# More buffers for key outputs and bias rows, the first gate loaded ahead of the last attention output, and the last merge parts moved forward on POOL

## The chip, the cores and the metric

The kernel runs on one core of a Trainium2 chip. The metric is the time of one launch on the device in microseconds (us). A core has five instruction queues that matter here: TensorE (PE, matmuls into PSUM banks), VectorE (DVE), ScalarE (ACT), GpSimd (POOL) and SyncE (SP, which here only issues transfers). Each runs its own list of instructions in order; semaphores tie them together. A tile with `bufs=n` has n buffers in turn, and whoever fills one again waits until the earlier use of that buffer is over, its transfer to memory included.

## The reference

One layer of a streaming encoder, for a new stream of 1024 frames and 64 more frames of a running one (1088 rows in all), in float32:

```
h = rms_norm(x, norm_w) @ w_in                    # 1024 -> 6144 columns
sb_q, sb_k, sb_v, sb_z, cb_q, cb_k, cb_v, cb_z, g_sb, g_cb = split(h)
o_sb = stick_breaking(sb_q, sb_k, sb_v)           # first branch, 8 heads x 64
o_cb = band_attention(cb_q, cb_k, cb_v, rel_bias) # second branch, 8 heads x 64
b_sb = (o_sb * silu(sb_z)) @ w_proj_sb
b_cb = (o_cb * silu(cb_z)) @ w_proj_cb
h = sigmoid(g_sb) * b_sb + sigmoid(g_cb) * b_cb   # the merge
y = x + h @ w_out
```

The new keys and values of both branches are outputs too.

## The kernel before, in words

Most float32 operands are split into two parts, a high part made by a copy on ACT to a shorter format (`whi`, `hl[:, 0]`, `og` with index 0) and a low part, the difference, made on DVE or POOL (`wlo`, `hl[:, 1]`, `og` with index 1). A product is then three matmuls: high by high, high by low, low by high. So each weight block goes through ACT and through DVE or POOL before PE can use it.

The work runs in five stages.

1. *First projection* (from L450), with frames on the partitions, for values and for the normalized queries and keys of the second branch. `make_rb` (L240) builds, in its eight calls, the bias rows of the eight heads: DVE writes a tile `rx` of 128 x 768 (L243, L244), and SP sends it to `d_rb` (L245). Between such calls DVE makes the low parts of the transposed queries and keys (L354), whose PSUM bank `pk` PE needs again (L349).
2. *Second projection* (L606 to L657), columns on the partitions, in pairs of weight blocks. Each pair takes seven products (s = 0 to 6) instead of eight, with sums of blocks (`s1`, `u2`, `u3`) added on DVE. `emit` (L565) splits a finished piece into `hl` and sends it to memory. For keys it also plans an `out` (L590): PE transposes the piece into a bank `acc` (L595, L597), ACT copies it into `ko` (L601) and, for the second column piece, into `kos` (L599), and SP sends both to the outputs. There are two `acc` banks, three `ko` and one `kos`. `soon(n, f)` puts f in a list, and `step` (L553), called once ahead of each product's matmuls, counts down and runs what has come due; with n = 1 that is the second `step` from there. The matmuls of a product are issued after `step`.
3. *Attention* of both branches, with the gate columns' projections put in as filling between steps (`fill`).
4. *Merge*. `proj_sb` (L855) multiplies the first branch's projection with its gate, and `proj_cb` (L894) does the same for the second branch in 12 jobs j: i, ci = divmod(j, 3), where i is the pair of weight blocks and ci one of three pieces of the frames (384, 384 and 320 columns). Before these jobs `load_og` (L822) fetches piece ci of the attention output (`ot`), and `make_og` (L842) splits it, four high parts on ACT (L834) and four low ones, alternately on POOL and DVE (L839). `load_gcb(j)` (L882) fetches gate j as two transfers of SP (L853), and `sig(j)` (L888) puts the sigmoid on ACT (L892, the first one loads the function table). Job j starts with `sig(j + 1)`, so that on ACT gate 1 stands ahead of the weights that are split after job 0 (L115 on ACT, L122 on DVE), which job 3 needs. After each job `keep_hi` (L931, on ACT, L937) and `keep_lo` (L939, on POOL, L945) split its result for the output projection. `sums_h` (L947) adds and splits pieces of the result (`tk`, L955 on ACT, L959 on DVE), for sums that the output projection multiplies.
5. *Output projection* (L1380 to L1463), again seven products in the order 0, 3, 2, 1, 4, "b", 5, 6. `prep_o` (L1243) splits its weights, on ACT (L1271) and POOL (L1272). `last_sums` (L1331), called while the first product runs, issues what is left of the merge: the remaining `sums_h`, the weights of the fourth product, and the parts of job 11. After them DVE adds results (L1432) and the rows of the running stream (L1449).

Of the kernel before, what the change touches and what calls it, by code (L numbers as in the profile page):

```python
# [32 lines left out]
def hybrid_step_kernel(ctx: ExitStack, tc: tile.TileContext, x_prompt, x_sample, c_sbk, c_sbv, c_cbk, c_cbv,  # L33
# [164 lines left out]
    with ExitStack() as ph:  # L198
# [40 lines left out]

        def make_rb(h):  # L240
            rb = rbs[0]
            rx = p1.tile([128, 768], F32, name="rx", bufs=2)
            V.tensor_scalar(rx[:, 0:512], rb[:, h, 256:257].to_broadcast([128, 512]), -1.0, None, op0=OP.mult)  # L243
            V.tensor_scalar(rx[:, 512:768], rb[:, h, 255::-1], -1.0, None, op0=OP.mult)  # L244
            SP.dma_start(d_rb[h], rx)  # L245
# [298 lines left out]
    with ExitStack() as ph:  # L544
# [5 lines left out]
        def soon(n, f):  # L550
            later.append([n, f])
# [13 lines left out]
        def emit(i, w, half, c, src, ps):  # L565

            kind, _, arg = pairs[i]
            n = XC[c][1] - XC[c][0]
            plain = lambda d, s: SP.dma_start(d, s)
            if kind in ("sig", "silu"):  # L570
                sg = up.tile([128, 2, 288], F32R, name="hl", bufs=HB)[:, 0].bitcast(F32)
                A.activation(sg[:, :n], src[:, :n], AF.Sigmoid)
                if kind == "silu":
                    V.tensor_tensor(out=sg[:, :n], in0=sg[:, :n], in1=src[:, :n], op=OP.mult)
                soon(0, lambda: stores(plain, half, c, sg[:, :n], arg[w][:]))
                return
            h = up.tile([128, 2, 288], F32R, name="hl", bufs=HB)
            A.activation(h[:, 0, :n], src[:, :n], AF.Copy)
            V.tensor_tensor(out=h[:, 1, :n], in0=src[:, :n], in1=h[:, 0, :n].bitcast(F32), op=OP.subtract)
            p = arg + w  # L580
            dst = (d_kT if kind == "k" else d_qT)["sb"][p]
            soon(0, lambda: stores(rdma, half, c, h[:, :, :n], dst[:]))
            if kind == "q":
                return
            kf = src
            if ps:
                kf = up.tile([128, 288], F32, name="kf", bufs=2)
                V.tensor_copy(kf[:, :n], src[:, :n])

            def out():  # L590
                pt = psF.tile([128, 512], F32, name="acc")
                ko = up.tile([128, 2, 128], F32, name="ko", bufs=3)
                cols = slice(p * 128, (p + 1) * 128)
                for t in range(2):
                    TE.transpose(pt[:, t * 128:(t + 1) * 128], kf[:, t * 128:(t + 1) * 128], ident)  # L595
                if c == 1:
                    TE.transpose(pt[:32, 256:384], kf[:, 256:288], ident)  # L597
                    kos = up.tile([32, 128], F32, name="kos", bufs=1)
                    A.activation(kos, pt[:32, 256:384], AF.Copy)  # L599
                    SP.dma_start(o_sbk_s[32 * half:32 * half + 32, cols], kos)  # L600
                A.activation(ko[:, :2], pt[:, :256].rearrange("p (t c) -> p t c", c=128), AF.Copy)  # L601
                a = half * 512 + c * 256
                SP.dma_start(o_sbk_p[a:a + 256, cols].rearrange("(t q) c -> q t c", q=128), ko[:, :2])
            soon(1, out)

        load_raw(2)  # L606
        for n in range(2, LEAD):
# [214 lines left out]
    def load_og(b, ci, stage, ps=range(NPAIR)):  # L822
        a, e = CH[ci]
        for p in ps:
            if b == "sb":
                ots[ci, p] = stage.tile([128, 384], F32, name="ot", bufs=4)
            elif p % 2 == 0:
                t = stage.tile([128, 2, 384], F32, name="ot", bufs=2)
                ots[ci, p], ots[ci, p + 1] = t[:, 0], t[:, 1]
            SP.dma_start(ots[ci, p][:, :e - a], d_o[b][p][:, a:e])  # L830
# [11 lines left out]
    def make_og(b, ci):  # L842
        for p in range(NPAIR):
            og_hi(b, ci, p)
            og_lo(b, ci, p)
# [36 lines left out]
    def load_gcb(j):  # L882
        if j < 12:
            i, ci = divmod(j, 3)
            load_gate(*((late["tbp"], "gt") if j % 4 < 2 else (late["y"], "ot")), ("cb", j),
                      (d_g["cb"][i], d_g["cb"][i + 4]), ci)

    def sig(j):  # L888
        if j < 12:
            a, e = CH[j % 3]  # L890
            t = gts["cb", j][:, :, :e - a]
            A.activation(t, t, AF.Sigmoid)  # L892
# [38 lines left out]
    def keep_hi(j):  # L931
        i, ci = divmod(j, 3)
        a, e = CH[ci]
        for u, z in ((i, 512), (i + 4, NP)):
            if a < min(e, z):
                hh, _, f = kept(u, a, min(e, z))
                A.activation(hh, f, AF.Copy)  # L937

    def keep_lo(j):  # L939
        i, ci = divmod(j, 3)  # L940
        a, e = CH[ci]
        for u, z in ((i, 512), (i + 4, NP)):
            if a < min(e, z):
                hh, hl, f = kept(u, a, min(e, z))
                G.tensor_tensor(out=hl, in0=f, in1=hh.bitcast(F32), op=OP.subtract)  # L945

    def sums_h(k):  # L947

        f, tk = late["tbt"], late["tk"][k]
        x = lambda h, c: f[:, k + 4 * h, 512 * c:512 * c + 512]  # L950
        d = [psF.tile([128, 512], F32, name="acc")[:] for _ in range(2)]

        def high(n):
            for j in range(2):
                A.activation(tk[:, 0, n + j], d[j], AF.Copy)  # L955

        def low(n):
            for j in range(2):
                V.tensor_tensor(out=tk[:, 1, n + j], in0=d[j], in1=tk[:, 0, n + j].bitcast(F32), op=OP.subtract)  # L959

        for j in range(2):
            V.tensor_tensor(out=d[j], in0=x(j, 1), in1=x(0, j), op=OP.subtract)
        high(0)
        yield
        low(0)
        V.tensor_tensor(out=d[1], in0=x(1, 1), in1=d[0], op=OP.subtract)
        V.tensor_tensor(out=d[0], in0=x(1, 0), in1=d[1], op=OP.subtract)
        yield
        high(2)
        yield  # L970
        low(2)
# [302 lines left out]

    late["o"] = prep_o
    for ci in range(3):
        load_og("cb", ci, late["y"])
        fill((46, 24, 100000)[ci])
        if ci == 2:
            for j in range(2):  # L1280
                load_gcb(j)
            late["h"][1] = [xpool.tile([128, 4, T], F32R, name=f"x{s}") for s in "ab"]
        make_og("cb", ci)
    sig(0)
    for j, q in enumerate(((0, 1), (1, 1), (0, 0))):
        SP.dma_start(wsum[j], w_quarter(0, *q))
    for j in range(2, 4):
# [43 lines left out]
    def last_sums():  # L1331
        for _ in tjobs:
            pass
        t3 = sums_h(3)
        for _ in range(3):
            next(t3)
        prep_o(3)
        keep_hi(11)
        keep_lo(11)
        for _ in t3:  # L1340
            pass
        late["ev"] = xpool.tile([128, 34, 256], F32, name="xm")
        late["ev"] = [late["ev"][:, 17 * j:17 * j + 17] for j in range(2)]
# [149 lines left out]
```

## Time and profile before

| what | value |
|---|---|
| time, median of 3 runs | 1016.16 us (1014.17 to 1017.79) |
| the profiled execution's own time | 1019.66 us |
| its span, first to last instruction | 1017.8 us |
| PE busy | 983.5 us, 97% of the span |
| DVE busy | 658.2 us, 65% |
| ACT busy | 474.2 us, 47% |
| POOL busy | 323.9 us, 32% |
| mean granted clock of PE | 0.993 |

A row of a timeline gives the start and the duration in us, the engine (SPq and ACTq are transfers issued), the line, the operation, the tiles it writes and reads, and in brackets how long the engine stood idle before it and what ended that. A row of the waits of PE reads: what waited, on what, total us, times, longest. A row of a window gives its bounds and length, the busy time of PE, of the weight loads (PEld), of DVE, ACT and POOL, each with its number of instructions, then the granted clock of PE as a share of full speed, the share of the DMA engines and GB/s.

### The profile page before, as it was taken

How to read it: one execution, taken by the hardware profiler on the slowest of the kernel's cores; microseconds unless marked ns; L12 is line 12 of the kernel's file. 1: busy time of each engine (PE TensorE's matmuls, PEld its weight loads, DVE VectorE, ACT ScalarE, POOL GpSimd, SP SyncE). 2: the span in 40 equal slices, each digit the busy share in tenths (PEclk: the TensorE clock that was granted, in tenths of full speed). 3: DMA queues.
4: the chain of work that ended last, by engine and by line, in shares of the span. 5: the costliest groups of instructions: out<-in, count | busy, mean ns of one | idle time of the engine just before them, and what ended most of it. 6: DMA issues, size and time to landing. Idle time of an engine off the chain costs nothing. (4 is left out here: it accounts for less than half of the span.)

```text
span 1017.8 us, 20166 instructions
## 1 busy us (share of the span) xinstructions
PE 983.5 (97%) x7512; PEld 935.4 (92%) x7512; DVE 658.2 (65%) x1233; ACT 474.2 (47%) x1075; POOL 323.9 (32%) x338
## 2 busy tenths in 40 slices
PE   6999999998999999999999999999999999899998
PEld 5999999998999999988888889898988898799998
DVE  5466663894455454199888877566766675588645
ACT  5544442343343433276667656444445443355220
POOL 3376663205354543211111101110103102375452
PEclk9999999999999999999999999999999999999999
DMA  7636467435556332786656554665667854852632
GB/s 239 213 114 206 174 244 278 126 94 155 178 159 178 102 96 84 198 213 181 163 153 164 144 146 126 175 205 150 175 159 213 248 174 148 257 159 70 192 124 97
DMA packets 180866, 169.83 MB, mean 167 GB/s; under 512 B 34913, under 2 KB 167137, under 8 KB 180641
## 3 DMA queue, kind: packets, MB, share of 16 engines
q1 hardware_dynamic: 172048, 160.23, 53.4%
q10 hardware_dynamic: 8720, 8.33, 2.6%
q8 instruction: 59, 0.97, 0.4%
q14 instruction: 39, 0.31, 0.1%
HBM read 109.78 MB, written 58.72 MB: 166 GB/s over the span
## 5 line engine op out<-in xcount | busy, mean ns | idle before, releaser
L122 POOL TENSOR_TENSOR wlo<-wraw,whi 128x1024 fp32r<-128x1024 f32 x30 | 73.8, 2459 | 247.5 <-ACT whi L115 227.0
L773 PE MATMUL acc<-xm,whi 128*128 128x384 f32 (+1 forms) x384 | 128.6, 335 | 0.0
L1044 DVE TENSOR_TENSOR_SCAN kp<-kp,imp 64x576 f32<-64x576 f32 (+8 forms) x72 | 102.7, 1427 | 21.4 <-ACT kp L1027 21.2
L1034 ACT ACTIVATE be<-be,sm 128x640 f32<-128x640 f32 (+5 forms) x72 | 50.8, 705 | 97.5 <-DVE sm L1030 97.5
L1076 PE MATMUL pt<-ident,be 128*128 128x128 f32 (+2 forms) x608 | 89.7, 271 | 6.3 <-DVE wT L1087 3.4
L1085 ACT ACTIVATE wT<-pt 128x512 f32<-128x512 f32 (+3 forms) x130 | 63.5, 502 | 54.9 <-PE pt L1076 54.7
L1076 PEld LDWEIGHTS pt<-ident,be 128*128 128x128 f32 (+2 forms) x608 | 68.2, 140 | 18.3 <-issue 6.4
L464 PE MATMUL acc<-whi,xa 128*128 128x256 f32 x256 | 74.2, 292 | 0.0
L773 PEld LDWEIGHTS acc<-xm,whi 128*128 128x128 f32 x384 | 72.5, 189 | 1.1
L464 PE MATMUL acc<-whi,xm 128*128 128x256 f32 x256 | 70.8, 278 | 0.0
L464 PE MATMUL acc<-wlox,xm 128*128 128x256 f32 x256 | 70.8, 278 | 0.0
L464 PE MATMUL acc<-wlo,xa 128*128 128x256 f32 x256 | 70.7, 278 | 0.0
L464 PE MATMUL acc<-whix,xb 128*128 128x256 f32 x256 | 70.7, 278 | 0.0
L464 PE MATMUL acc<-whix,xm 128*128 128x256 f32 x256 | 70.6, 278 | 0.0
L1115 PE MATMUL o<-wT,vp 128*64 128x256 f32 (+1 forms) x608 | 66.6, 360 | 0.0
L1045 DVE TENSOR_TENSOR be<-be,kp 64x576 f32<-64x576 f32 (+8 forms) x72 | 60.3, 837 | 9.6
L1027 ACT ACTIVATE kp<-z 128x384 f32<-128x384 f32 (+6 forms) x112 | 54.2, 484 | 24.4 <-PE z L1025 22.9
L773 PE MATMUL acc<-xa,wlo 128*128 128x384 f32 (+1 forms) x192 | 65.4, 341 | 0.0
L773 PE MATMUL acc<-xa,whi 128*128 128x384 f32 (+1 forms) x192 | 65.3, 340 | 0.0
L773 PE MATMUL acc<-xm,wlo 128*128 128x384 f32 (+1 forms) x192 | 65.1, 339 | 0.0
L1115 PEld LDWEIGHTS o<-wT,vp 128*64 128x64 f32 x608 | 42.7, 138 | 23.4 <-issue 8.0
L773 PE MATMUL acc<-xb,whi 128*128 128x384 f32 (+1 forms) x192 | 64.0, 334 | 0.0
(298 smaller groups left out, 3028.1 us busy)
## 6 DMA issues: line engine op xcount, KB each, us to landing
wraw<-in_w_in_dram SPq DMA_DIRECT2D x35, 512.0 KB, 4.5
wrawx<-in_w_in_dram SPq DMA_DIRECT2D x13, 512.0 KB, 4.3
sq<-d_qsbT SPq DMA_DIRECT2D x32, 192.0 KB, 4.4
sq<-d_qcbT SPq DMA_DIRECT2D x32, 192.0 KB, 4.0
gt<-d_gsb SPq DMA_DIRECT2D x30, 192.0 KB, 3.3
xt<-in_x_prompt_dram SPq DMA_DIRECT2D x8, 512.0 KB, 5.2
d_kcbT<-hl SPq DMA_DIRECT2D x8, 512.0 KB, 4.4
d_qcbT<-hl SPq DMA_DIRECT2D x8, 512.0 KB, 5.6
```

What stands on the lines that cost most here:

```text
L122: (eng or G).tensor_tensor(out=l, in0=raw, in1=h[:].bitcast(F32), op=OP.subtract)
L464: TE.matmul(ps, x, w, start=m == 0, stop=m == len(steps) - 1)
L773: TE.matmul(ps[:, :b - a], w[:, k], xk(x, k)[:, a:b], start=k == 0 and n == 0, stop=k == KT - 1 and n == 2)
L1027: A.activation(kp[:r, x:y], z[:r, :m], AF.Sigmoid, scale=-0.125)
L1034: A.activation(be[:r, :n], be[:r, :n], AF.Exp, bias=kp[:r, j:j + 1], scale=-1.0, accum_out=kp[:r, 2:3])
L1044: V.tensor_tensor_scan(kp[:r, n - 1::-1], kp[:r, n - 1::-1], im[:, ::-1], 0.0, op0=OP.mult, op1=OP.add)
L1045: V.tensor_tensor(out=be[:r, :n], in0=be[:r, :n], in1=kp[:r, 1:n + 1], op=OP.mult)
L1076: TE.transpose(pt[:kr, x, :r], be[:r, kb * 128:kb * 128 + kr], ident[:r, :r])
L1085: A.activation(w[:, sl:sl + m, q0:q0 + r], pt[:, :m, :r], AF.Copy)
L1115: TE.matmul(o[hd * 64:hd * 64 + 64, c0:c1], vv[:kr, kb, hd * 64:hd * 64 + 64], wT[b, p, j, hd, s // 4][:kr, s % 4, c0:c1], start=si == 0, ...
```

## The change

Four edits:

```
-            rx = p1.tile([128, 768], F32, name="rx", bufs=2)
+            rx = p1.tile([128, 768], F32, name="rx", bufs=3)
...
-                ko = up.tile([128, 2, 128], F32, name="ko", bufs=3)
+                ko = up.tile([128, 2, 128], F32, name="ko", bufs=4)
...
-                    kos = up.tile([32, 128], F32, name="kos", bufs=1)
+                    kos = up.tile([32, 128], F32, name="kos", bufs=2)
...
-            soon(1, out)
+            soon(2 if (w, half) == (0, 1) else 1, out)
...
     for ci in range(3):
-        load_og("cb", ci, late["y"])
+        if ci < 2:
+            load_og("cb", ci, late["y"])
         fill((46, 24, 100000)[ci])
         if ci == 2:
-            for j in range(2):
-                load_gcb(j)
+            load_gcb(0)
+            load_og("cb", ci, late["y"])
+            load_gcb(1)
             late["h"][1] = [xpool.tile([128, 4, T], F32R, name=f"x{s}") for s in "ab"]
+            sig(0)
         make_og("cb", ci)
-    sig(0)
...
     def last_sums():
         for _ in tjobs:
             pass
+        keep_hi(11)
+        keep_lo(11)
         t3 = sums_h(3)
         for _ in range(3):
             next(t3)
         prep_o(3)
-        keep_hi(11)
-        keep_lo(11)
         for _ in t3:
             pass
```

First, `rx` gets a third buffer. Second, `ko` gets a fourth and `kos` a second one, and the `out` of the piece (w, half) = (0, 1), which is finished by the seventh product of a pair, is put off by one more `step`. Third, for the last piece of the second branch's attention output, gate 0 is fetched ahead of it and gate 1 behind it, and the sigmoid of gate 0 is put ahead of the split of that piece. Fourth, the split of job 11's result comes first in `last_sums`, after what was left of the earlier sums.

The second edit on PE, at the passage from one pair of the second projection to the next. `u_3327` and `u_3342` are the two pieces finished last by the pair before; `b_3607` is the bank of the new pair's first product (s = 0), the bank filled from `t1h` and `t1l` that of its second (s = 1), `b_3680` that of its third. Before:

```order
L634 MATMUL b_3607<-xm,whi 128x288
L634 MATMUL b_3607<-xa,whi 128x288
L595 MATMUL acc<-ident,u_3327 128x128 x2
L595 MATMUL acc<-ident,u_3342 128x128 x2
L597 MATMUL acc<-ident,u_3342 32x128
L634 MATMUL b_3643<-t1h,wlo 128x256
L634 MATMUL b_3643<-t1l,wlo 128x256
```

Now:

```order
L634 MATMUL b_3642<-t1l,wlo 128x288
L634 MATMUL b_3642<-t1h,wlo 128x288
L595 MATMUL acc<-ident,u_3327 128x128 x2
L595 MATMUL acc<-ident,u_3342 128x128 x2
L597 MATMUL acc<-ident,u_3342 32x128
L634 MATMUL b_3680<-t0h,whix 128x256
L634 MATMUL b_3680<-t0l,whix 128x256
```

The five transposes stood between the first and the second product and now stand between the second and the third.

The third edit on ACT, at the end of attention and the start of the merge's second branch. `og` are the high parts of the attention output, four for each piece, `gt` gates, and the last `whi` the weights for job 3:

```order
 L834 ACTIVATE og_11226<-ot 128x384 x8
+L892 ACT_TABLE_LOAD
+L892 ACTIVATE gt<-gt 128x768
 L834 ACTIVATE og_11226<-ot 128x320 x4
-L892 ACT_TABLE_LOAD
-L892 ACTIVATE gt<-gt 128x768 x2
+L892 ACTIVATE gt<-gt 128x768
 L115 ACTIVATE whi<-wraw 128x1024
```

The table load and gate 0 have moved ahead of the third piece's four parts; gate 1 has stayed between them and the weights. On SP the two transfers of gate 0 have likewise moved ahead of the third piece's four.

The fourth edit on POOL, at the start of the output projection. `xb` is the low part of job 11's result, the `wo` weights of the third and of the fourth product. Before:

```order
L1272 TENSOR_TENSOR wlo<-wraw,whi 128x1024
L1329 TENSOR_TENSOR hs<-xm,hs 128x8x64
L1272 TENSOR_TENSOR wo_11951<-wo_11215,wo_11950 128x1024
L1272 TENSOR_TENSOR wo_11995<-wo_11214,wo_11994 128x1024
L945 TENSOR_TENSOR xb<-xm,xa 128x256
L1272 TENSOR_TENSOR wlo<-qraw,whi 128x1024
```

Now:

```order
L1272 TENSOR_TENSOR wlo<-wraw,whi 128x1024
L1331 TENSOR_TENSOR hs<-xm,hs 128x8x64
L1272 TENSOR_TENSOR wo_11951<-wo_11215,wo_11950 128x1024
L945 TENSOR_TENSOR xb<-xm,xa 128x256
L1272 TENSOR_TENSOR wo_11997<-wo_11214,wo_11996 128x1024
L1272 TENSOR_TENSOR wlo<-qraw,whi 128x1024
```

The split of job 11's result has changed places with the weights of the fourth product. On ACT its high part has moved ahead of four `tk` copies (L955) and of those weights' high part.

## The prediction, made before the changed kernel had run

> **What bounds the kernel now.** I began with the busy time of each engine, went on to the waits of TensorE (PE) with what ended each, then to the granted clock in short windows, and last to the timeline around each wait. The first part of the page:
>
> ```profile
> PE 983.5 (97%) x7512; PEld 935.4 (92%) x7512; DVE 658.2 (65%) x1233; ACT 474.2 (47%) x1075; POOL 323.9 (32%) x338
> ```
>
> PE is busy for 983.5 of 1017.8 us, so an edit that leaves its arithmetic alone can win only PE's idle time and whatever time it computes slowly. The other engines have room on the average, which says nothing of a single stage. The waits of PE, with total, number and longest:
>
> ```profile
> PE acc L595 <- ACT ko L601: 4.3, 2, 3.0
> ...
> PE b L917 <- DVE wlo L122: 3.1, 1, 3.1
> ...
> PE b L1407 <- DVE fl L1449: 2.2, 1, 2.2
> ...
> PE b L917 <- ACT whi L115: 1.6, 1, 1.6
> ...
> PE pk L349 <- DVE hl L354: 1.1, 1, 1.1
> ```
>
> Five of these rows lie where the change works: the transposes of keys (L595, two waits), the merge's fourth job (L917, two waits), the start of the output projection's second position (L1407), and the bias rows, if `hl` is late because of them (L349). The rows left out lie at the start, in attention and elsewhere outside the change. The five add up to 4.3 + 3.1 + 1.6 + 2.2 + 1.1 = 12.3 us. Next, windows of about 3.4 us, two stretches, with PE's busy time and the granted clock (PEclk):
>
> ```profile
> 883.20:886.60 3.40, 0.91 (x4) 0.33 (x3) 3.17 (x5) 2.74 (x5) 1.32 (x1) 1.00 1.08 362
> 886.64:890.05 3.41, 1.29 (x4) 1.29 (x5) 3.38 (x3) 0.74 (x1) 3.41 (x3) 0.50 0.83 239
> 890.05:893.47 3.42, 3.42 (x13) 3.42 (x12) 3.10 (x5) 2.72 (x5) 3.42 (x4) 0.50 0.62 186
> 944.66:948.08 3.42, 1.39 (x11) 1.39 (x12) 2.52 (x5) 0.38 (x1) 0.00 (x0) 1.00 0.46 153
> 948.08:951.50 3.42, 3.42 (x19) 3.42 (x18) 1.07 (x2) 2.02 (x3) 0.00 (x0) 0.50 0.79 175
> ```
>
> After a window in which PE worked 0.91, 1.29 or 1.39 us, the next one has a clock of 0.50, though PE works all through it. So the merge's wait and the L1407 wait cost more than their own length. The Trainium skill's page "TensorE: Matmul & The Clock Gate", Part 1, puts the fall at an idle window of about 3.4 us and gives "no PE-idle gaps >~3.4µs" as the practical limit; by that none of the waits above would touch the clock and the gain could not pass their plain sum. The rows disagree, since a window with 1.39 us of work was enough, and the measurement decides.
>
> **The change part by part.** The sum is made against the profiled execution, 1019.66 us (span 1017.8 and 1.9 around it), which is 3.5 us above the median of the runs, 1016.16.
>
> *A third buffer for bias rows.* DVE's row:
>
> ```profile
> 159.35 0.43 DVE L243 TENSOR_SCALAR rx<-ck 128x512 f32<-128x512 f32 x1 [2.78 <-DMA d_rb<-rx]
> ```
>
> VectorE stood 2.78 us for a transfer out of the older of two buffers, and `hl` (L354), for which PE waits 1.1 us, is queued behind it. Three transfers now have to be under way before this can happen. PE's gain can't be more than its wait, and the next lender of delay is ScalarE's half of `hl`; I take 1.1, bounds 0 and 1.1.
>
> *Key outputs.* ACT's and PE's rows around the longer wait:
>
> ```profile
> 252.94 0.27 ACT L599 ACTIVATE kos<-acc 32x128 f32<-32x128 f32 x1 [3.25 <-DMA out_dram<-kos]
> 253.11 0.36 ACT L601 ACTIVATE ko<-acc 128x256 f32<-128x256 f32 x1
> 253.73 0.42 ACT L578 ACTIVATE hl<-u 128x256 fp32r<-128x256 f32 x1 [0.27 <-DMA d_ksbT<-hl]
> ...
> 256.30 0.36 ACT L601 ACTIVATE ko<-acc 128x256 f32<-128x256 f32 x1
> ```
> ```profile
> 253.52 0.44 PE L595 MATMUL acc<-ident,s 128*128 128x128 f32 x2 [3.00 <-ACT ko L601]
> ...
> 256.92 0.60 PE L595 MATMUL acc<-ident,u 128*128 128x128 f32 x4
> ...
> 260.46 0.28 PE L634 MATMUL b<-t0h,whix 128*128 128x256 f32 x1
> ```
>
> The single `kos` waits 3.25 us for its own transfer to the output; behind it on ACT stands the `ko` that frees the PSUM bank. With two `kos` and four `ko` both copies run at about 249.7, and PE goes on at once. What is late next on ACT is the `hl` at 253.73: it waits for a transfer of its own, which this change doesn't hasten, and the two `ko` behind it end at 256.66 at the latest. PE, 3.0 us earlier, would reach the transposes of 256.92 at 253.9 and wait there some 2.7 us; that is what the move answers. They now come after the next products, which end at 260.46 in the old time, 3.5 us after 256.92 with 0.4 us of transposes taken off, 3.1. So PE gets there at 257.0, and the bank is free at 256.66. The move adds one wait: the second new `u` of DVE (L642) takes the buffer that the delayed transposes read, so it waits for them, some 0.4 us; nothing that PE needs within the next products hangs on it. The second wait, 1.3 us, is the same case a pair later. Gain 4.3; bounds 1.6 (the move doesn't cover, 2.7 come back) and 4.3.
>
> *Gate ahead of the last attention output.* ACT, SP, the landing times of the gate tiles (`gt`) in this stage, and PE:
>
> ```profile
> 881.19 1.28 ACT L892 ACT_TABLE_LOAD   x1 [3.77 <-DMA gt<-d_gcb]
> 882.48 1.58 ACT L892 ACTIVATE gt<-gt 128x768 f32<-128x768 f32 x2
> 883.97 1.04 ACT L115 ACTIVATE whi<-wraw 128x1024 fp32r<-128x1024 f32 x1
> ```
> ```profile
> 869.96 0.80 SPq L853 DMA_DIRECT2D gt<-d_gsb  x2
> 872.60 2.09 SPq L830 DMA_DIRECT2D ot<-d_ocb  x4
> 874.74 1.87 SPq L853 DMA_DIRECT2D gt<-d_gcb  x4
> ```
> ```profile
> DMA to landing us min/median/max: 2.2/3.5/6.0
> ```
> ```profile
> 879.82 0.45 PE L917 MATMUL b<-og,whi 128*128 128x320 f32 x2
> ...
> 883.19 0.30 PE L917 MATMUL b<-og,wlo 128*128 128x320 f32 x1
> ...
> 893.61 0.34 PE L917 MATMUL b<-og,wlo 128*128 128x384 f32 x1
> 893.79 0.51 PE L917 MATMUL b<-og,whi 128*128 128x384 f32 x2
> 894.13 0.34 PE L917 MATMUL b<-og,wlo 128*128 128x384 f32 x1
> ```
>
> At full clock a matmul of this shape takes 0.52 / 3 = 0.173 us (893.61 to 894.13). Between 883.19 and 893.61 lie 17 others, so 18 steps should have taken 3.1 us and took 10.4: this place costs 7.3, of which 4.7 are the two waits and 2.6 the clock. The chain: gate 0 lands, table load, gate 0, gate 1, the weights' high part (`whi`), and on DVE their low part. After the change gate 0 is issued right behind the first branch's gates, at 870.8, and by the median of 3.5 is in at 874.3; the table load and gate 0 (1.28 + 0.8) end at 876.4, in time that ACT otherwise spends waiting for the third output. Gate 1 has gate 0's old place in SP's queue. It should then land when gate 0 did, 881.19. From there: 0.8 for gate 1 (half of 1.58), 1.04 for `whi`, so 883.0 instead of 885.0, about when PE asks for it. The low part:
>
> ```profile
> 885.50 3.20 DVE L122 TENSOR_TENSOR wlo<-wraw,whi 128x1024 fp32r<-128x1024 f32 x1
> 950.57 1.23 DVE L1272 TENSOR_TENSOR wlo<-xm,whi 128x1024 fp32r<-128x1024 f32 x1 [2.35 <-ACT whi L1271]
> ```
> ```profile
> 885.28 2.35 POOL L1297 TENSOR_TENSOR wo<-wo,wo 128x1024 f32<-128x1024 f32 x1 [7.34 <-DMA wo<-in_w_out_dram]
> ```
>
> The same subtraction took 3.20 us where POOL's L1297 had begun 0.22 before it and 1.23 where POOL stood still. From 883.0 it would be through at 884.3, before POOL's weights land at 885.28. PE wants it at 883.19 + 0.15 + 2 x 0.173 = 883.7, so about 0.6 is left, too short to halve a clock by the rows above; POOL's parts for the sixth job become late next, for which I leave 0.4 by estimate. Gain 7.3 - 1.0 = 6.3. The bounds are 1.3 (POOL first, below) and 7.3.
>
> *Last parts of the merge first.* POOL, DVE and ACT, and two stretches of PE from the chain that ended last:
>
> ```profile
> 940.93 2.40 POOL L1272 TENSOR_TENSOR wo<-wo,wo 128x1024 fp32r<-128x1024 f32 x1 [5.52 <-ACT wo L1271]
> 943.29 0.73 POOL L945 TENSOR_TENSOR xb<-xm,xa 128x256 fp32r<-128x256 f32 x1
> ```
> ```profile
> 944.06 1.29 DVE L1432 TENSOR_TENSOR xm<-b,xr 128x512 f32<-128x512 f32 x2 [3.32 <-POOL xb L945]
> ```
> ```profile
> 933.19 0.60 ACT L955 ACTIVATE tk<-acc 128x512 fp32r<-128x512 f32 x1 [0.53 <-DVE acc L962]
> ```
> ```profile
> 946.69 12.82 PE b L1407 x96
> ...
> 966.76 10.88 PE b L1407 x96
> ```
>
> DVE waits 3.32 us for the last POOL part, which itself stands behind a 2.40 us weight step; PE waits 2.18 us behind DVE and then does 96 matmuls in 12.82 us where the same 96 take 10.88 later, so 1.94 more go to the clock. Together 4.1. Moved ahead, the ACT part (0.4 us) fits into the 0.53 us for which ACT stood before 933.19, and POOL's 0.73 into the 5.52 us it stood before 940.93. DVE, which had nothing else to wait for since 944.06 - 3.32 = 940.74, can then pass up to 3.3 earlier, more than PE's 2.18. Cost: `tk` copies up to 0.4 later if ACT's slot is missed. What is late next is the weight step at 940.93, which ends 943.3, 1.2 before PE stops now. Gain 4.1, bounds 2.2 (clock halved all the same) and 4.1.
>
> The sum: 1.1 + 4.3 + 6.3 + 4.1 = 15.8, so 1003.9 for an execution like the profiled one. Against the median the same sum gives 1000.4. About 4.5 us of it is clock loss, which hangs on where the 3.4 us windows fall, so that the timed runs may have lost a little less of it; I take 0.6 off and predict 1001.0.
>
> **The rivals.**
>
> *POOL begins its w_out sum before DVE's split.* If the w_out transfer lands two us earlier, or gate 1 two us later, or each by one, L122 runs beside L1297 again: 3.2 instead of 1.23, and PE stands some 2.6 us once more with half a clock behind it. C then keeps about 1.3 to 2 of its 6.3: 1001.0 + 4.5 = 1005.5. For it speaks that the margin is 2.3 us (883.0 to 885.28) and that both depend on transfers; against it, that SP issues the w_out transfers no earlier than before. The Trainium skill's "SBUF — State Buffer", section "SBUF: two separate sides", calls the port pair that DVE and POOL share an exclusive lock, held for the whole instruction by whoever starts first; by it L122 would have waited until 887.63 and then taken its 1.23, 3.36 in all. The trace agrees: 3.20.
>
> *The waits go, the clock stays.* If halved windows come from something else than the gaps before them, only the plain waits return: 1016.16 - 12.3 + 1.0 = 1004.9. The rows above speak against it: each of the three halved windows follows a mostly idle or halved one.
>
> *Two more buffers that don't reach the wait.* ACT's next transfer wait (`hl`, 253.73) may take the place of the `kos` one, and B falls to 1.6: 1003.7. Similarly D may only move its wait to DVE's sums.
>
> *Slower.* ACT's queue is in order, and the third output's four parts now stand behind the table load and gate 0. If gate 0 is late, PE waits at the third job, which starts at 879.82. Table load, gate 0 and about 1.3 for the first part of that output make 3.4, so gate 0 has to be in by 876.4, and each us beyond costs one; to eat 15.8 and 3 more it would have to land near 895, 24 us after its issue, where the longest of these transfers took 6.0 (876.8, a loss of 0.4). The place is right for a loss, the price isn't.
>
> **How the numbers follow.** Forecast 0.68; POOL first 0.17; clock stays or B or D half 0.10; no effect (each wait taken over by the next one) 0.03; slower 0.02. Under about 0.3% (3 us) a measurement of this kernel can't be told from no change. The low end takes C and the clock in full and 3 us for the scatter of the runs: 997. The high end takes POOL first (1005.5) with B at 1.6 (2.7 more): 1008. Faster 0.95, same 0.03, slower 0.02.
>
> **What would show it.** Right: no L595 wait on `ko`, no `rx` wait of more than 1 us, L122 on DVE near 1.2 us and ahead of L1297, L945 (128x256) before the weight step, and no window at 0.50 near 887 to 893 and 948. Wrong: L122 at 3.2 us again; a new PE wait on `og` at the third job; `hl` L578 on ACT with 2 us and PE behind it at the moved transposes.

## The result, and the profile after

The changed kernel takes 1000.62 us (median of 4 runs, 999.05 to 1001.92), the kernel before 1015.71 (4 runs, 1014.17 to 1017.79): a ratio of 0.9849, 95% interval 0.9826 to 0.9873. The forecast was 1001.0, faster; the whole interval lies below 1, so the kernel is faster, by 1.5%. The profiled execution of the changed kernel took 1001.92 with a span of 1000.1, so against the profiled one of before (1019.66) it is 17.7 us shorter, where the medians lie 15.1 apart. That difference of 2.6 us comes up again at the end.

The waits of PE, in the same columns as before:

```profile
PE pt L277 <- DVE xn L266: 8.1, 2, 7.4
PE pt L1076 <- DVE wT L1087: 3.4, 3, 2.4
PE pt L1076 <- ACT wT L1085: 2.4, 3, 1.3
PE acc L464 <- ACT whi L115: 2.1, 1, 2.1
PE z L1024 <- DVE sm L1030: 1.4, 2, 1.0
PE acc L873 <- DVE xm L877: 0.5, 1, 0.5
PE pt L1076 <- DVE be L1045: 0.5, 1, 0.5
```

All five rows of the prediction (L595, L917 twice, L1407, L349) are gone, and no row has come in their place. What is left lies at the start, in attention and, with 0.5 us (L873), in the first branch's merge. The merge's second branch and the output projection, before and after, from the first matmul to the last:

```profile
871.49:926.10 54.61, 49.96 (x290) 49.38 (x289) 44.23 (x57) 30.14 (x53) 34.23 (x28) 0.94 0.55 167
926.18:1013.92 87.74, 85.55 (x738) 85.15 (x736) 53.42 (x64) 23.16 (x31) 38.73 (x17) 0.98 0.43 136
```
```profile
865.29:912.60 47.31, 47.31 (x290) 47.31 (x289) 41.10 (x56) 29.00 (x52) 32.38 (x26) 1.00 0.62 192
912.65:996.26 83.61, 83.60 (x738) 83.41 (x736) 52.93 (x66) 23.58 (x33) 40.83 (x18) 1.00 0.45 142
```

After the change PE is busy for the whole of both (47.31 of 47.31, 83.60 of 83.61) at a clock of 1.00; before it stood or ran at half clock for 7.3 and 4.1 us more.

The third edit's chain, on ACT, DVE and POOL (the changed kernel's POOL sum is L1299, two lines further down than before):

```profile
868.66 1.28 ACT L892 ACT_TABLE_LOAD   x1 [2.57 <-DMA gt<-d_gcb]
869.96 0.85 ACT L892 ACTIVATE gt<-gt 128x768 f32<-128x768 f32 x1
870.71 1.74 ACT L834 ACTIVATE og<-ot 128x320 fp32r<-128x320 f32 x4
874.15 0.85 ACT L892 ACTIVATE gt<-gt 128x768 f32<-128x768 f32 x1 [1.70 <-DMA gt<-d_gcb]
874.91 1.04 ACT L115 ACTIVATE whi<-wraw 128x1024 fp32r<-128x1024 f32 x1
```
```profile
875.99 1.23 DVE L122 TENSOR_TENSOR wlo<-wraw,whi 128x1024 fp32r<-128x1024 f32 x1 [0.30 <-ACT whi L115]
```
```profile
877.67 2.41 POOL L1299 TENSOR_TENSOR wo<-wo,wo 128x1024 f32<-128x1024 f32 x1 [4.47 <-DMA wo<-in_w_out_dram]
```

The table load and gate 0 lie in ACT's time before the third output; the weights' low part takes 1.23 us and is through at 877.22, 0.45 before POOL's sum begins. Counted from the branch's first matmul, 865.29, it is through after 11.9 us (877.22); before it was after 17.2 (885.50 + 3.20 - 871.49).

The stages side by side, in us, from the traces. Each is counted from the start of its first matmul, the first and third row to the start of the last one, the other two to its end:

| stage | before | after | shorter by | forecast |
|---|---|---|---|---|
| bias rows and transposes (L349) | 112.80 | 111.50 | 1.30 | 1.1 |
| second projection (L634) | 178.06 | 172.57 | 5.49 | 4.3 |
| merge, second branch (L917) | 54.55 | 47.22 | 7.33 | 6.3 |
| output projection (L1407) | 87.73 | 83.60 | 4.13 | 4.1 |

They add up to 18.25; the stages between took 0.6 more in this execution.

These are two executions. The experiments below give more of both kernels, and where an experiment leaves a stage alone, its trace shows how far that stage differs by execution:

| stage | kernel before, number of executions | changed kernel, number of executions |
|---|---|---|
| bias rows and transposes | 112.7 to 112.9, 5 | 111.5, 8 |
| second projection | 176.5 to 178.1, 5 | 172.4 to 173.1, 7 |
| merge, second branch | 49.0 to 55.0, 4 | 47.2 to 47.8, 7 |
| output projection | 87.2 to 87.7, 3 | 83.6, 8 |

No execution of the kernel before reaches the changed kernel's time in any of the four.

### The profile page after: what moved, and what is told of

Same layout as the page of the kernel before. It is cut to its first block, busy times and chain, and to the rows that moved or that the text cites. A ratio compares the mean times of both kernels' runs of the same rounds, so it can differ in the third digit from the quotient of the medians.

```text
span 1000.1 us, 20177 instructions
## 1 busy us (share of the span) xinstructions
PE 977.8 (98%) x7512; PEld 930.8 (93%) x7512; DVE 657.0 (66%) x1233; ACT 472.9 (47%) x1075; POOL 324.9 (32%) x338
## 4 chain that ended last, share of the span: by engine, by line
PE 92%; DMA 2%; DVE 2%; ACT 1%; SPq 1%; issue 1%; POOL 1%; DVEq 0%; ACTq 0%
PE acc L464 19%; PE acc L773 18%; PE b L634 17%; PE b L1409 8%; PE o L1115 7%; PE pt L1076 6%; PE b L917 5%; PE z L1025 3%; PE z L1024 3%; PE acc L873 3%; PE pk L349 1%; DMA wrawx<-in_w_in_dram 1%; DMA gt<-d_gsb 1%; DVE be L1045 1%; PE pt L277 1%
## 5 line engine op out<-in xcount | busy, mean ns | idle before, releaser
L122 POOL TENSOR_TENSOR wlo<-wraw,whi 128x1024 fp32r<-128x1024 f32 x30 | 74.2, 2473 | 243.9 <-ACT whi L115 209.2
L1076 PE MATMUL pt<-ident,be 128*128 128x128 f32 (+2 forms) x608 | 90.1, 272 | 6.4 <-DVE wT L1087 3.4
L1076 PEld LDWEIGHTS pt<-ident,be 128*128 128x128 f32 (+2 forms) x608 | 68.5, 140 | 18.4 <-issue 6.4
```

The source lines that it names most:

```text
L122: (eng or G).tensor_tensor(out=l, in0=raw, in1=h[:].bitcast(F32), op=OP.subtract)
L1076: TE.transpose(pt[:kr, x, :r], be[:r, kb * 128:kb * 128 + kr], ident[:r, :r])
```

## The experiments

*Theory:* each edit removes one wait of PE, and the half clock behind it, where there was one, and the four don't depend on one another. *Rivals:* the wait is covered or replaced by another one (named at each); the clock falls for other reasons; the place that the profile showed is a matter of that one execution. The kernels made for this section were timed once each, all but the last, and single times say little here, since the kernel before alone took 1009.04 to 1019.80 us in 11 runs. So each experiment is read by the length of its stage in its trace.

**The bias rows: two buffers again.**

```
-            rx = p1.tile([128, 768], F32, name="rx", bufs=3)
+            rx = p1.tile([128, 768], F32, name="rx", bufs=2)
```

> The changed kernel with two bias-row buffers again. Theory: DVE waits some 2.8 us at the bias row near 156 to 159 us and PE's wait of 1.1 us for hl (L349) is back, so the first stage is longer by 1.1 to 1.3 us and nothing else changes. Rival (the wait was no more than chance in the transfers): DVE's wait is of another length and PE's stage is as in the changed kernel.

The stage takes 112.78 us again, 1.28 longer than after the change, and DVE's wait is back:

```profile
159.08 0.43 DVE L243 TENSOR_SCALAR rx<-ck 128x512 f32<-128x512 f32 x1 [2.77 <-DMA d_rb<-rx]
```

PE's row is back too, with the length that it had before:

```profile
PE pk L349 <- DVE hl L354: 1.1, 1, 1.1
```

So it went as the theory has it. The other three stages stayed within 0.6 us of the changed kernel's.

**The key outputs: buffers without the move, and the move with one `kos`.**

```
-            soon(2 if (w, half) == (0, 1) else 1, out)
+            soon(1, out)
```

> The changed kernel, with the delayed transposes put back to their old place ahead of the second product, all buffers kept. Theory (the two edits need each other): the wait of 3.0 us on kos stays gone, but PE now comes to the transposes right after the first product, where both acc banks are still full because ACT stands at hl behind hl's own transfer; a wait of PE on ko (L595) of about 2 to 2.5 us appears at the first passage between pairs and of about 2 at the second, so the second projection's stage loses 4 of the 5.5 us that it had gained. Rival (the buffers alone do it, the move is idle): no L595 wait of over 0.3 us, stage as in the changed kernel.

The second projection takes 176.82 us, 4.25 of the 5.49 are lost again. ACT and PE of this run:

```profile
251.58 0.42 ACT L578 ACTIVATE hl<-u 128x256 fp32r<-128x256 f32 x1 [2.23 <-DMA d_ksbT<-hl]
253.62 0.44 ACT L578 ACTIVATE hl<-u 128x288 fp32r<-128x288 f32 x1 [1.62 <-DMA d_ksbT<-hl]
254.49 0.36 ACT L601 ACTIVATE ko<-acc 128x256 f32<-128x256 f32 x1
```
```profile
249.32 0.60 PE L595 MATMUL acc<-ident,s 128*128 128x128 f32 x4
254.91 0.85 PE L595 MATMUL acc<-ident,u 128*128 128x128 f32 x4 [1.91 <-ACT ko L601]
```

At 249.32 PE goes on without a wait, thanks to the buffers; at the next transposes it stands 1.91 us, since ACT is held up twice by the transfers of `hl` and frees the bank only at 254.85. This is the next wait that the prediction named, and without the move it takes most of the gain. (The two waits, 1.91 and 1.77 us, are a little shorter than expected.) The other half of the pair:

```
-                    kos = up.tile([32, 128], F32, name="kos", bufs=2)
+                    kos = up.tile([32, 128], F32, name="kos", bufs=1)
```

> The changed kernel with one kos again, four ko and the delayed transposes kept. Theory (kos is the buffer that was short): ACT waits about 3 us for the transfer out of kos, PE waits about 3.0 and 1.3 us on ko at the same two places as in the kernel before, and the stage loses 4.3 to 5. Rival (ko was the short one, or the move covers it): no such waits, stage as in the changed kernel.

177.63 us, 5.05 lost. With the move and four `ko`, but one `kos`, ACT's old wait and PE's old row return:

```profile
PE acc L595 <- ACT ko L601: 4.7, 2, 2.8
```

```profile
251.03 0.27 ACT L599 ACTIVATE kos<-acc 32x128 f32<-32x128 f32 x1 [3.00 <-DMA out_dram<-kos]
```

So neither half is worth much alone: `kos` was the short buffer and the move covers what is late next.

**The gate made late.** ACT's order as changed, but gate 0's transfers back behind those of the third output:

```
-            load_gcb(0)
             load_og("cb", ci, late["y"])
+            load_gcb(0)
             load_gcb(1)
```

> The changed kernel with gate 0's transfers back behind those of the last attention output, while the sigmoid of gate 0 keeps its new place on ACT ahead of that output's split. It is the slower rival's mechanism made to happen. Theory: gate 0 lands some 10 us later than in the changed kernel (near 875 there), the four og parts of the third piece stand behind it on ACT, PE waits for og at the third job some 4 to 5 us (one us for each us of lateness beyond 876.4 on the old time axis), and the clock halves for one or two windows behind that, so that the merge's second branch takes 5 to 9 us more than in the changed kernel, about as long as before the change or longer. Rival (the gate's place in the queue does not matter, the order on ACT alone won): less than 1 us more.

The branch takes 52.37 us, 5.15 more than in the changed kernel. The table load starts 8.50 us after the branch's first matmul, where it started 3.37 after it; 5.13 later. PE and the two windows there:

```profile
875.59 0.41 PE L917 MATMUL b<-og,whi 128*128 128x320 f32 x1 [2.55 <-ACT og L834]
876.53 0.41 PE L917 MATMUL b<-og,whi 128*128 128x320 f32 x1 [0.53 <-POOL og L839]
```
```profile
873.50:876.90 3.40, 0.78 (x3) 0.56 (x4) 0.97 (x2) 3.39 (x7) 1.29 (x2) 1.00 0.93 312
876.90:880.30 3.40, 3.40 (x15) 3.40 (x14) 3.33 (x6) 2.08 (x4) 3.40 (x3) 0.50 0.67 205
```

The slower rival's mechanism is real: the third output stands behind a late gate on ACT, PE waits 3.1 us for it, and the clock halves behind that. In this execution its price is near one us for one. It was the place of the transfers in SP's queue that made it harmless in the changed kernel. The gate was less late than expected (5 us, not 10), the loss is at the lower end.

**POOL's sum made early.** The three w_out transfers ahead of gate 1's:

```
+            for j, q in enumerate(((0, 1), (1, 1), (0, 0))):
+                SP.dma_start(wsum[j], w_quarter(0, *q))
             load_gcb(1)
...
-    for j, q in enumerate(((0, 1), (1, 1), (0, 0))):
-        SP.dma_start(wsum[j], w_quarter(0, *q))
```

> The changed kernel, with the three w_out transfers issued ahead of gate 1's, so that POOL's first w_out sum can begin earlier and gate 1 comes later. Theory (first rival of the prediction made to happen): the weights are in about 1 us earlier, gate 1 about 2 us later, L1299's sum starts before DVE's L122, L122 takes over 2.5 us, PE waits 2 to 4 us for it at job 3 and the clock halves behind that, so that the branch loses 3 to 6 of the 7.3 us. Rival (there is enough room): L122 stays at 1.2 us and the branch loses less than 1.5.

The branch takes 54.06 us, 6.84 more, but not by the theory's road. PE of this run:

```profile
880.39 1.01 PE L917 MATMUL b<-og,whi 128*128 128x384 f32 x2 [3.42 <-ACT whi L115]
```

Gate 1, issued at 869.50, had landed only at 878.45, behind 1.5 MB of weights; POOL's sum was over by then (876.04 to 878.39), and L122 took 1.22 us from 880.37. So the loss is that of a late gate 1. The loss is somewhat more than the theory's 3 to 6 us and came by another road, so this run says nothing for a collision.

**POOL's sums made late, on the kernel before.**

```
-        if j == 1:
+        if j == 4:
             G.tensor_tensor(out=wsum[3], in0=wsum[0], in1=wsum[1], op=OP.add)
-        if j == 2:
+        if j == 5:
             G.tensor_tensor(out=wsum[2], in0=wsum[3], in1=wsum[2], op=OP.subtract)
-        if j:
+        if j == 2:
+            keep_lo(1)
+            keep_lo(0)
+        elif j > 2:
             keep_lo(j - 1)
```

> The kernel before, with only POOL's two w_out sums moved from jobs 1 and 2 of the merge to jobs 4 and 5, and the split of job 0's result put behind that of job 1's, so that POOL has nothing to do while DVE makes the low part of the weights for job 3. All transfers and ACT's order stay. Theory (DVE's 3.20 us is one third own work and two thirds waiting for POOL): L122 on DVE takes 1.2 to 1.3 us, PE's wait on it falls from 3.08 to about 1.1, one of the two half-clock windows there goes, and the merge's second branch is 3 to 3.7 us shorter than before, half of the 7.3 that the changed kernel won there. Rival (the long subtraction comes from DMA traffic or from the tiles): L122 stays near 3.2 us and nothing is won.

L122 took 1.22 us and the branch 48.18, 6.4 less than before, more than the theory allowed. There is a second difference, which the edit doesn't make: gate 0's table load started 7.46 us after the branch's first matmul, in the profiled execution of before 9.70, and L122 11.77 after it. The executions below have POOL's sum at 12.62 to 13.90, so L122 would probably have come first anyway. This run alone can't settle it; it raised the question of the next one.

**The kernel before, twice more.**

> The kernel before, unchanged, profiled once more. The question: is the collision of DVE's L122 with POOL's L1297 in the merge (3.20 us, 7.3 us lost there in all) a property of the kernel or of one execution? Theory (which of the two starts first is decided by transfers that differ from one execution to the next by some us): gate 0 is in 7 to 10 us after the first matmul of the branch, L122 takes 1.2 us where it starts before L1297 and up to 3.5 where it starts after; the branch takes 48 to 49.5 us from its first matmul to its last in the one case, 52 to 55 in the other, against 47.2 in the changed kernel. Rival (it is fixed): L122 again 3.2 us and 54.5 us for the branch.

> The kernel before, unchanged, a further execution; the same two theories with the same numbers. The rest (waits of 2.8 to 3.0 and 0 to 1.6 us for ko, 1.1 for hl at L349, 2.2 to 2.9 at the output projection) should come again, and the number of half-clock windows should differ between the executions by where the 3.41 us windows fall.

Together with the run described next, whose code is that of before up to the output projection, this makes four executions of the same merge, in us after the branch's first matmul:

| execution | table load | L122 starts, takes | POOL's sum starts, takes | branch |
|---|---|---|---|---|
| before, profiled | 9.70 | 14.01, 3.20 | 13.79, 2.35 | 54.55 |
| once more | 9.76 | 14.08, 3.25 | 13.90, 2.34 | 55.04 |
| a third time | 8.66 | 12.97, 3.19 | 12.74, 2.35 | 52.65 |
| the next experiment | 8.27 | 12.58, 1.22 | 12.62, 3.44 | 48.98 |
| changed kernel | 3.37 | 10.70, 1.23 | 12.38, 2.41 | 47.22 |

Besides the merge, the waits that were expected came again at L349 (1.2 and 1.0 us) and at the output projection (2.18 in both). For `ko` PE waited 3.02 and 1.31 us in the first repetition, as expected, but only 1.45, 0.30 and 1.23 in the second.

The fourth row of the table tells most, with these two lines:

```profile
882.42 1.22 DVE L122 TENSOR_TENSOR wlo<-wraw,whi 128x1024 fp32r<-128x1024 f32 x1
```
```profile
882.46 3.44 POOL L1297 TENSOR_TENSOR wo<-wo,wo 128x1024 f32<-128x1024 f32 x1 [6.45 <-DMA wo<-in_w_out_dram]
```

and beside it the second:

```profile
884.61 3.25 DVE L122 TENSOR_TENSOR wlo<-wraw,whi 128x1024 fp32r<-128x1024 f32 x1
```
```profile
884.43 2.34 POOL L1297 TENSOR_TENSOR wo<-wo,wo 128x1024 f32<-128x1024 f32 x1 [7.70 <-DMA wo<-in_w_out_dram]
```

Where DVE began 0.04 us earlier, DVE took 1.22 and POOL 3.44; where POOL began 0.18 earlier, POOL took 2.34 and DVE 3.25. The one that starts second pays nearly the whole of the other. This is what the Trainium skill's "SBUF — State Buffer" (section "SBUF: two separate sides") calls an exclusive lock held for the instruction, and these runs agree with it in both directions. So the 7.3 us of the profiled execution were not fixed: of these four executions, three lost 5.4 to 7.8 against the changed kernel, one 1.8. The change brings L122 1.7 us ahead of POOL's sum in the profiled execution, and 1.0 to 2.3 us in the seven that keep its merge as it is.

**Matmuls put into the idle time at the output projection.** On the kernel before, 16 matmuls that nobody reads, in addition to the work:

```
+            if n == 2:
+                fi = psF.tile([128, 512], F32, name="acc")
+                for k in range(16):
+                    TE.matmul(fi[:, :256], hs[:, k % 8], oblk_last[0][:, k % 4], start=True, stop=True)
+            oblk_last = wh, wl
```

> The kernel before, with 16 matmuls of 128x256 that nobody reads put into the idle time of PE ahead of the product that waits for the last merge part (2.18 us; 16 of them take 1.8). The wait itself stays: the product starts when it did. Theory (the half clock comes from the idle time before it): no half-clock window behind it, the 96 matmuls after it take about 10.9 us in place of 12.8, so the output projection is about 1.9 us shorter although PE does more work. Rival (the clock falls there for another reason): a window of 0.50 at the same place, 96 matmuls in 12.8 us, no gain or a small loss.

```profile
932.97 2.15 PE L1402 MATMUL acc<-whi,hs 128*128 128x256 f32 x16 [1.12 <-DVE tk L959]
```

There is no half-clock window behind, but also no gain: the stage takes 88.02 us (before 87.73). The matmuls had come one half product too early: they waited 1.12 us for their own bank and took 1.8, and with PE 3 us later the wait for L1449 was over when PE got there. Besides, PE's steps were longer for a while, of which more below. The wait was moved, not filled, and the run doesn't separate wait and clock. The first repetition of the kernel before does that by chance. There the same wait of 2.18 us lay across the border of two windows:

```profile
941.20:944.61 3.41, 2.84 (x26) 2.64 (x24) 1.02 (x2) 0.00 (x0) 2.36 (x2) 1.00 0.00 0
944.61:948.03 3.42, 1.81 (x15) 1.81 (x16) 2.24 (x4) 0.38 (x1) 0.00 (x0) 1.00 0.50 163
948.03:951.44 3.41, 3.41 (x32) 3.41 (x31) 1.33 (x2) 2.42 (x3) 0.28 (x1) 1.00 0.85 236
```

PE worked 2.84 and 1.81 us in them, and the next window kept its full clock (32 matmuls in 3.41 us, where the halved one of the prediction did 19).

**The fourth edit undone.**

```
+        t3 = sums_h(3)
+        for _ in range(3):
+            next(t3)
+        prep_o(3)
         keep_hi(11)
         keep_lo(11)
-        t3 = sums_h(3)
-        for _ in range(3):
-            next(t3)
-        prep_o(3)
```

> The changed kernel with the last merge parts back behind the third sum and its weights, as before; everything else stays changed. Theory (the fourth edit stands by itself): DVE waits 3.3 us for the last POOL part, PE waits 2.2 to 2.9 us for the running stream's rows at the output projection, and from its first matmul to its last the output projection takes 87.2 to 87.9 us in place of 83.60, with a half-clock window or without. Rival (the earlier and smoother merge hides it): under 1 us of wait, 83.6 to 84.6.

```profile
932.18 5.73 PE L1409 MATMUL b<-wo,tk 128*128 128x256 f32 x48 [2.18 <-DVE fl L1451]
```

DVE's wait (3.32) and PE's (2.18) are back to the hundredth, and the output projection takes 86.46 us, 2.86 more than in the changed kernel; no window halved in it. The edit stands by itself, as the theory has it, but the forecast of 87.2 to 87.9 was too high. What the same wait costs differs by execution: 2.9 here and 3.6 in the first repetition of the kernel before (87.16), both without a half clock, 4.1 in the profiled execution and the second repetition (87.73 and 87.69), both with one. The 0.7 beyond the wait can be followed in the starts of PE's matmuls in this trace. Where nothing holds PE up, one starts 0.113 us after the one before it (48 in 5.44 us, in the chain that ended last). At the wait two starts lie 2.46 us apart and the next two 0.22. At the next weights, which the chain that ended last has coming from ACT (L1271), two lie 0.40 apart, 0.12 of it a second wait, and the next two 0.19:

```profile
938.03 0.47 PE L1409 MATMUL b<-whi,tk 128*128 128x256 f32 x2
```

These four steps are 2.82 longer than steady ones, which is nearly the whole of the 2.86. So the first wait cost 2.45 for its 2.18, and the rest belongs to the second. In the first repetition of the kernel before the same four steps make 2.8 of 3.6. Most of the rest built up over about 20 us in which the matmuls followed each other at 0.118 us, at a granted clock of 1.00; the chain that ended last has both kinds:

```profile
958.92 5.65 PE b L1407 x48
977.52 5.44 PE b L1407 x48
```

The runs with the 16 added matmuls and with POOL's sums late show the longer steps too, for about 33 and 18 us. I have no cause for them.

**A further place of the same kind.** In both kernels the longest wait that the change leaves, apart from the start of the kernel, is one of 2.40 us (L1076 for the copy L1087). In the changed kernel it has this in front of it:

```profile
572.09 2.64 DVE L1045 TENSOR_TENSOR be<-be,kp 64x576 f32<-64x576 f32 x1
574.65 0.67 DVE L1087 COPY wT<-pt 128x512 f32<-128x512 f32 x1
575.25 1.34 DVE L1044 TENSOR_TENSOR_SCAN kp<-kp,imp 64x576 f32<-64x576 f32 x1
576.73 0.75 DVE L1045 TENSOR_TENSOR be<-be,kp 64x576 f32<-64x576 f32 x1
```
```profile
571.59 2.52 POOL L122 TENSOR_TENSOR wlo<-wraw,whi 128x1024 fp32r<-128x1024 f32 x1 [10.85 <-ACT whi L115]
```

The same product takes 2.64 us beside POOL's split and 0.75 without. First that split on DVE:

```
-                            W.split(("u", j + 1) if j + 1 < len(units) else ("p", 0))
+                            W.split(("u", j + 1) if j + 1 < len(units) else ("p", 0), V if j == 7 else G)
```

> The changed kernel with one weight split of the attention stage (the low part that POOL makes in 2.5 us near 572 us) made on DVE instead. POOL then does nothing while DVE multiplies 64x576 (2.64 us in the changed kernel). Theory (while POOL and DVE both read two operands from SBUF, the one that starts second waits for the whole of the first): the product takes 0.75 us as elsewhere, the split 1.23 behind it, the copy that PE waits for comes about 0.7 us earlier and PE's wait falls from 2.40 to about 1.7. Rival (the product is slow because of its tiles or of transfers): it still takes over 2 us, and with the split behind it PE waits 3.5 us or more.

```profile
571.48 0.75 DVE L1045 TENSOR_TENSOR be<-be,kp 64x576 f32<-64x576 f32 x1
572.16 1.21 DVE L122 TENSOR_TENSOR wlo<-wraw,whi 128x1024 fp32r<-128x1024 f32 x1
573.29 0.67 DVE L1087 COPY wT<-pt 128x512 f32<-128x512 f32 x1
```

0.75 us with POOL idle: product and split one behind the other on DVE (1.9 us together) are faster than the product alone beside POOL's split (2.64). PE waited 0.23 us for ACT's copy and, four transposes later, 0.76 for DVE's, better than the 1.7 expected. The one run took 997.91 us. Then, in the changed kernel instead, the copy that PE waits for on ACT:

```
-                if flip[0] % 2 or b == "sb" and flip[0] % 4:
+                if flip[0] % 2 or b == "sb" and flip[0] % 4 or flip[0] == 76:
```

> The changed kernel with one more edit, in attention: the one copy of transposed weights (L1087, 128x512) that DVE makes behind a product of 2.64 us, while POOL makes the low part of a weight block (L122, 2.5 us), is made on ACT, which stands idle then. DVE's product of that shape takes 0.75 us elsewhere. Theory: PE's wait of 2.40 us near 573 us falls to 0.5 to 0.8, the half-clock window behind it goes, and the time is 3 to 3.6 us under the changed kernel's, near 997.3. Rival (the transposes also wait for something else, or a later copy on DVE becomes late): the wait stays over 1.5 us or moves, and the gain is under 1 us.

997.20 us (6 runs, 996.18 to 997.40), where the kernel before, on the same chip, took 1015.39 (11 runs): a ratio of 0.9826, interval 0.9799 to 0.9854. DVE's product still takes 2.65, PE waits 0.23, and no window halves there:

```profile
573.20 1.14 PE L1076 MATMUL pt<-ident,be 128*128 128x128 f32 x8 [0.23 <-ACT wT L1085]
```

Against the changed kernel's 1000.62 this is 3.4 less, as forecast, though the two medians were not taken side by side. It is the shortest median of this study.

## Why the prediction was right, point by point

*Bias rows.* Right in place and size (1.1 forecast; 1.30 in the traces, 1.28 by undoing it). DVE still waits for `rx` with three buffers, 0.70 us where it waited 2.78 and 3.23 us later in the stage (164.51); PE doesn't notice. So the sign that I named for this part, no `rx` wait of over 1 us, did not come, though the gain did.

*Key outputs.* Right in mechanism, a little small in size: 4.3 forecast, 4.9 at the two passages. The forecast counted the waits alone, and a stop costs PE 0.2 to 0.3 us beyond its wait, as the steps at the output projection show (2.45 for 2.18); here there were two stops. The remaining 0.6 of the stage's 5.49 built up slowly over the last 90 us and isn't this edit's work: the second half of the stage takes 86.6 us in four of five executions of the kernel before and in one of the changed kernel (the one with the copy on ACT), 86.0 in all others, whichever kernel. So the run without the move, which has the 86.0, keeps 0.6 of the 4.9 at the passages, less than the lower bound of 1.6: there PE waits at both passages (1.91 and 1.77 us), where the bound has 2.7 at the first alone. And where the first `ko` wait of the kernel before was short (1.4 and 0.3 to 0.4 us in two executions), this edit is worth 3.9.

*Gate.* The steps of the chain came as worked out. Counted from the branch's first matmul, gate 0 was in after 3.4 us (forecast 874.3 - 871.49 = 2.8), gate 1 after 8.9 (forecast 9.7), and L122 began after 10.7 (forecast 11.5) and took 1.23. So the 1.0 us that I left over for a late L122 and for POOL's parts did not occur, gate 1 being 0.8 earlier. But the term rested on one execution, and by execution of the kernel before it is 1.8 to 7.8 us against the changed kernel's 47.22.

*Last parts.* Right for the profiled execution, 4.1 and 4.13; by execution it is 2.9 to 4.1, with the half clock at the upper end.

*The step that was off* is the last one, from the profiled execution to the median. I took 0.6 off; the profiled execution lost 2.6 us more to the same places than the median does (17.7 against 15.1). The terms were 1.9 too small together against the profiled execution, and this discount was 2.0 too small, so that two errors cancel and 1001.0 agrees with 1000.62 better than its parts do: that much of the agreement is luck. What makes the kernel before scatter (1009.0 to 1019.8 in 11 runs, against 996.2 to 997.4 for the best version) is, as far as the traces show, whether DVE or POOL comes first in the merge, how long PE waits for `ko`, and how many windows halve: four ahead of the end in the profiled execution, three in each repetition, one in the changed kernel, none in the best version. The 11 runs bear out the part of the windows: at a mean granted clock of 0.993 they took 1016.60 to 1019.80 us, at 0.995 1013.97 to 1016.61, at 0.997 and 0.998 1009.04 to 1012.25. The profiled execution, at 0.993, was one of the long ones.

*Rivals.* "POOL first" was the right thing to fear: it is what happened in three of four executions of the kernel before. In the changed kernel it did not happen in any of the seven executions that kept gate 0 early and the order of the transfers, by margins of 1.0 to 2.3 us. "The clock stays" is refuted by the windows of the changed kernel. "Buffers that don't reach the wait" is right for either half of the second edit alone. "Slower" was made to happen and cost 5.15, far from the 19 that it would have needed.

## What to carry to other kernels

A wait of the bound engine is worth its length plus, where it empties most of a window, the half clock behind it; both show in the profile, and the second varies with the execution. The restart adds 0.2 to 0.3 us in these traces. Ask for each wait removed what is late next on the same in-order engine: here buffers alone kept about an eighth of the gain (0.6 of 4.9 us). A DVE row that takes twice its time or more should be laid beside POOL's rows of the same microseconds before anything else is blamed, and an instruction that PE waits for should be moved away from that place, to another engine or ahead.

## What the runs showed of the hardware that was not expected

- Of two operations on 128x1024 with two operands each, one on DVE and one on POOL, that begin within 0.2 us of each other, the second pays: DVE 1.22 and POOL 3.44, or DVE 3.25 and POOL 2.34; alone 1.23 and 2.4. In attention a 64x576 product of 0.75 us took 2.64 in the same way.
- At the output projection a window in which PE worked 1.39 of 3.41 us was followed by a halved one, a window with 1.81 was not. The same wait of 2.18 us at the output projection was followed by a halved window in two executions and by none in two others, by where the window's border fell. PE's busy time alone doesn't give one limit for all stages: in the run with one `kos` a window with 1.53 us of work in the second projection was followed by one at full clock, and in the run with the fourth edit undone one with 1.71 in attention by a halved one:

```profile
249.73:253.14 3.41, 1.53 (x13) 1.52 (x14) 0.79 (x2) 0.98 (x4) 0.00 (x0) 1.00 0.55 154
253.14:256.56 3.42, 3.42 (x30) 3.42 (x29) 1.06 (x2) 3.24 (x9) 1.99 (x2) 1.00 0.77 230
```
```profile
790.68:794.09 3.41, 1.71 (x11) 1.10 (x9) 2.96 (x9) 1.35 (x3) 0.56 (x1) 1.00 0.94 289
794.09:797.51 3.42, 3.42 (x15) 3.42 (x16) 2.58 (x10) 1.24 (x3) 0.00 (x0) 0.50 1.03 282
```

- At a granted clock of 1.00 PE's matmuls of 128x256 followed each other at 0.113 us in most places and at 0.118 for 18 to 33 us behind a wait at the output projection in three executions. The second half of the second projection took 86.0 us in some executions and 86.6 in others, also at a clock of 1.00. The cause stays open.
